# A mixture-of-experts layer takes its tokens by indirect DMA instead of one-hot products

## The chip, the cores and the metric

The kernel runs on one core of one Trainium2 chip. The metric is device time in microseconds (us) of one execution; lower is better. The core has TensorE (PE, with its weight load PEld), VectorE (DVE), ScalarE (ACT), GpSimd (POOL), SyncE (SP) and 16 DMA engines. Each engine works through its own queue in order.

## The reference, cut to what matters

Two transformer blocks with 512 tokens of width 1024 end in a mixture of experts: 32 experts of hidden width 256, and each token goes to two of them. The part that the change touches is this:

```python
g_sel = top_k(g_logits, 1)                       # one of 4 groups
top_val, top_idx = top_k(e_logits_sel, 2)        # two of its 8 experts
gates = sum(one_hot(e_idx, 32) * e_weight)       # 512 x 32
...
a = einsum('nd,edf->nef', hf, w_g); u = einsum('nd,edf->nef', hf, w_u)
hid = silu(a) * u * gates
out = out + einsum('nef,efd->nd', hid, w_d)
```

All inputs are float32. Experts read 100 MB of weights, so each weight passes through the core once.

## The kernel before, in words

The kernel works in float32 accuracy with faster products: each operand is split into a high part (rounded on ACT, line 259, tiles `whi`) and a low part (the rest, on DVE, line 260, tiles `wlo`), three buffers each. Weights come as a stream of 512 KB pieces, called half units here (128 x 1024 floats), issued by SP (lines 234, 241 and 253). An expert has six of them: four for up and gate (`expert_up`, products at line 1589, 128x512) and two for down (`expert_down`, lines 266 to 268).

An expert handles up to `CAP` = 64 tokens. Experts go in groups of `EB` = 4, and in a group in two pairs; a pair fills 128 rows. Eight groups follow one another. For each group, `take(e)` prepares the tokens one group ahead. `gather` compares a table of ranks with a ramp and so writes a one-hot matrix `oh` (DVE, line 1557). It then multiplies the 512 normalised tokens, high and low part, by `oh` on PE: 64 products of 256 columns at line 1569. ACT copies each result from PSUM into `xg`, where the high and the low half of an expert's tokens lie side by side (line 1571, eight copies a group). `slots` multiplies `oh` by a small table `gcol` to learn the token number and the gate of each slot (PE line 1369, then five small DVE steps; the last, line 1382, writes the row numbers `sr` as integers). Those row numbers serve the output: `add_rows` scales the result by the gate and POOL adds it to rows of `out` in DRAM by an indirect DMA (line 1494), two a group.

Between these, `expert_hidden` folds the high and low products (line 1597), applies silu (ACT line 1599) and the product with `u` (DVE line 1600, `hid`); `expert_turn` transposes `hid` on PE (line 1609).

The order within each engine is fixed when the kernel is built, by a scheduler that interleaves the steps which Python yields. A weight tile is loaded as soon as its buffer is free, in the order of the SP queue. `fetch` sets how many half units may be in memory: `RING` = 11 buffers of their own, four in tiles of the residual, and five in pairs of half-size temporaries (line 241), 20 in all. A half unit in two half-size tiles is split by two ops of 512 columns on ACT and two on DVE.

Of the kernel before, what the change touches and what calls it, by code (L numbers as in the profile page):

```python
# [19 lines left out]
D = 1024  # L20
# [33 lines left out]
RING = 11  # L54
# [146 lines left out]
class Ker:  # L201
# [1039 lines left out]
    def route_begin(self):  # L1241
# [3 lines left out]
        for t, name in zip(self.rc, ("w_r", "tri", "b_r", "rdesc")):  # L1245
# [6 lines left out]
                   for n, j in enumerate(XORDER)}  # L1252
        self.ss, self.nr = None, 0

    def route_part(self, k, h):
# [12 lines left out]
        for i in range(NT):  # L1268
            nc.scalar.copy(self.xt[2 * i + k // 4][:, k % 4 * 128:(k % 4 + 1) * 128], pt[:, i * 128:(i + 1) * 128])

    def route(self, p, keep, mid):
# [38 lines left out]
        xt = [{}, {}]  # L1310
        for n, j in enumerate(XORDER):
            xt[0][j] = self.p_x.tile([128, T], F32R, name=("xh", "xl")[n // 4])[:, :512]
            nc.scalar.activation(xt[0][j], self.xt[j], AF.Copy, scale=y[:, 1 + j // 2:2 + j // 2])

        def lows():
            for n, j in enumerate(XORDER):
                xt[1][j] = self.p_x.tile([128, T], F32R, name=("xl", "xh")[n % 2])[:, :512]
                i = V.scalar_tensor_tensor(xt[1][j], self.xt[j], y[:, 1 + j // 2:2 + j // 2], xt[0][j].bitcast(F32), op0=OP.mult,
                                           op1=OP.subtract)
                if n == 0:  # L1320
                    self.tc.keep_in_program_order(i)

        return xt, lows, (lg, gm, og, m1, o1, m2, o2)

    def gating(self, p, found, gall, gcol):
# [29 lines left out]
        V.memset(gcol.bitcast(F32), 0.0)  # L1355
        V.tensor_copy(gcol[:, :, :, 0], self.slot[:, 0:4, None].to_broadcast([128, 4, NEXP // 2]))
        V.tensor_copy(gcol[:, :, :, 1:3], g2)
        V.tensor_sub(gcol[:, :, :, 3:5], g2, gcol[:, :, :, 1:3].bitcast(F32))

    def slots(self, pe, oh, gcol, e):  # L1360


        nc = self.nc
        V = nc.vector
        n = EB // 2
        ps = self.psb()
        for b in range(n):
            for i in range(NT):
                nc.tensor.matmul(ps[:, b * 8:b * 8 + 6], oh[:, i, b * 128:(b + 1) * 128], gcol[:, i, e // 2 + b, :], start=i == 0,
                                 stop=i == NT - 1, skip_group_check=True)  # L1370
        p3 = ps[:, :n * 8].rearrange("p (a b) -> p a b", a=n)
        g = pe.tile([128, n], F32, name="sg")
        t = pe.tile([128, n], F32, name="st")
        r = pe.tile([128, n], I32, name="sr")
        s = pe.tile([128, n, 8], F32, name="sp")
        V.tensor_copy(s[:, :, :5], p3[:, :, :5])
        for j in range(2):
            rows = slice(j * CAP, (j + 1) * CAP)
            V.tensor_add(g[rows], s[rows, :, 1 + j], s[rows, :, 3 + j])
        V.tensor_scalar(t, s[:, :, 0], 0.0, self.slot[:, 4:5], op0=OP.is_equal, op1=OP.mult)  # L1380
        V.scalar_tensor_tensor(t, s[:, :, 0], -1.0, t, op0=OP.add, op1=OP.add)
        V.tensor_copy(r, t)
        return r, g

    def moe(self):
# [3 lines left out]
        with ExitStack() as es:  # L1389
# [5 lines left out]
            gcol = pk.tile([128, 4, NEXP // 2, 6], F32R, name="gcol")  # L1395
# [3 lines left out]
            for n in range(4):  # L1399
# [3 lines left out]
                if n < 2:  # L1403
                    xs.append(pk.tile([128, 8, EB, 2, CAP], F32R, name=f"xg{n}"))
# [24 lines left out]
            xt, lows, found = self.route(pr, (rank, cmax), to_rows)  # L1429
# [20 lines left out]
            for j in range(RING + 4):  # L1450
                fetch(j)
            list(take(0))
            for j in range(RING + 4, RING + 9):
                fetch(j)
# [29 lines left out]
            self.overflow(pe, cmax, rank, gall, xt, xs, hh, out)  # L1484
# [12 lines left out]
    def overflow(self, pe, cmax, rank, gall, xt, xs, hh, out):  # L1497
# [3 lines left out]
        with tc.If(cnt > CAP):  # L1501
# [5 lines left out]
            with tc.For_i(0, NEXP, 1) as e:  # L1507
                with tc.For_i(CAP, S, CAP) as b:
                    oh, steps = self.gather(pe, rank[:, :, bass.ds(e, 1)], iota[:, bass.ds(b, CAP)], xt, xs[0])
                    list(steps)  # L1510
# [39 lines left out]
    def gather(self, pe, rank, iota, xt, x, lows=None):  # L1550

# [7 lines left out]
        if lows:  # L1559
            lows()  # L1560

        def steps():
            for part, src in enumerate(xt):
                for k in range(0, 8, 2):
                    pg = self.psb()
                    for j in range(2):
                        sl = slice((k + j) % 4 * 128, (k + j) % 4 * 128 + 128)
                        for i in range(NT):
                            nc.tensor.matmul(pg[:, j * m:(j + 1) * m], src[2 * i + k // 4][:, sl], oh[:, i, :m], start=i == 0,  # L1569
                                             stop=i == NT - 1, skip_group_check=True)  # L1570
# [549 lines left out]
```

## Time and profile before

| | us |
|---|---|
| median of three runs | 1752.95 (1751.96 to 1754.55) |
| the profiled execution | 1755.02 |
| its span, first to last instruction | 1753.1 |
| PE busy in the span | 1705.3 (97%) |
| DVE busy | 1090.5 (62%) |
| ACT busy | 861.0 (49%) |
| POOL busy | 59.1 (3%) |

Busy shares are means over stages that differ. The expert layer fills the last 310 us of the span, from about 1435 us on; its own shares have to be read from that stretch alone.

### The profile page before, as it was taken

The page shows a single profiled execution, that of the slowest core. Times are in us where ns is not written, and L with a number is a line of the kernel's source. Part 1 is how long each engine was busy: PE and PEld are TensorE (multiplying, and loading weights), DVE is VectorE, ACT ScalarE, POOL GpSimd, SP SyncE. Part 2 cuts the span into 40 slices and gives each one's busy share as a digit, 9 for nine tenths or more (in the row PEclk, how much of TensorE's full clock was granted, in tenths as well). Part 3 has the DMA queues.
Part 4 walks back from the last instruction along what each step waited for, and adds up shares of the span by engine and source line. Part 5 has one row for each costly group of instructions (what it writes and reads, how often), then busy time and mean ns, then how long its engine had stood idle before and what let it go on. Part 6 is the DMA issues. An engine that isn't in the chain of part 4 may idle for free.

```text
span 1753.1 us, 26914 instructions
## 1 busy us (share of the span) xinstructions
PE 1705.3 (97%) x10674; PEld 1497.2 (85%) x10674; DVE 1090.5 (62%) x1885; ACT 861.0 (49%) x1419; POOL 59.1 (3%) x65
## 2 busy tenths in 40 slices
PE   8999999999999999999999999999999999999996
PEld 8999999999999999878888888767767788888884
DVE  7678675633434344553434345589857768999995
ACT  6455654432323134441314144454346359999995
POOL 0000000000000000000000000100000000101102
PEclk9999999999999999999999999999969999999998
DMA  5211113232323222133333234322201458999993
GB/s 189 72 49 49 37 37 105 86 96 85 96 86 96 86 96 74 59 96 97 96 95 92 90 96 143 114 61 72 73 13 55 172 213 299 323 341 358 354 363 89
DMA packets 72339, 223.72 MB, mean 128 GB/s; under 512 B 9464, under 2 KB 9520, under 8 KB 72208
## 3 DMA queue, kind: packets, MB, share of 16 engines
q1 hardware_dynamic: 68976, 215.70, 36.7%
q0 software_dynamic: 3232, 6.25, 1.9%
q8 instruction: 85, 1.39, 0.3%
q14 instruction: 46, 0.38, 0.1%
HBM read 213.50 MB, written 12.60 MB: 129 GB/s over the span
## 4 chain that ended last, share of the span: by engine, by line
PE 91%; DVE 5%; ACT 2%; DMA 1%; issue 1%; SPq 0%; POOL 0%; POOLq 0%; DVEq 0%
PE pm L289 32%; PE ps L289 29%; PE ps L1589 6%; PE ps L1569 3%; PE ps L266 3%; PE ps L267 2%; PE ps L268 2%; PE ps L557 2%; DVE wlo L260 1%; PE ps L2060 1%; PE ps L2035 1%; PE ps L2053 1%; PE pm L485 1%; PE ps L1192 1%; DVE acc L1835 1%
## 5 line engine op out<-in xcount | busy, mean ns | idle before, releaser
L259 ACT CAST whi<-wraw 128x1024 fp32r<-128x1024 f32 (+1 forms) x309 | 321.3, 1045 | 606.1 <-PE pm L289 293.0
L260 DVE TENSOR_TENSOR wlo<-wraw,whi 128x1024 fp32r<-128x1024 f32 (+1 forms) x309 | 373.1, 1216 | 40.9 <-ACT whi L259 30.6
L289 PE MATMUL pm<-xh,whi 128*128 128x264 f32 x976 | 202.1, 288 | 8.4 <-ACT whi L259 6.0
L289 PE MATMUL pm<-xh,wlo 128*128 128x264 f32 x976 | 200.7, 286 | 0.5 <-DVE wlo L260 0.5
L289 PE MATMUL pm<-xl,whi 128*128 128x264 f32 x976 | 200.4, 287 | 0.1
L289 PE MATMUL ps<-xh,whi 128*128 128x512 f32 x472 | 191.8, 407 | 0.0
L289 PE MATMUL ps<-xh,wlo 128*128 128x512 f32 x472 | 186.1, 395 | 0.0
L289 PE MATMUL ps<-xl,whi 128*128 128x512 f32 x472 | 185.3, 393 | 0.0
L289 PEld LDWEIGHTS pm<-xh,whi 128*128 128x128 f32 x976 | 152.7, 190 | 9.4 <-ACT whi L259 6.0
L289 PEld LDWEIGHTS pm<-xh,wlo 128*128 128x128 f32 x976 | 152.4, 189 | 0.8 <-DVE wlo L260 0.7
L289 PEld LDWEIGHTS pm<-xl,whi 128*128 128x128 f32 x976 | 152.0, 189 | 0.7 <-DVE xl L467 0.6
L289 PEld LDWEIGHTS ps<-xh,whi 128*128 128x128 f32 x472 | 89.1, 189 | 23.5 <-issue 1.8
L289 PEld LDWEIGHTS ps<-xh,wlo 128*128 128x128 f32 x472 | 89.0, 189 | 21.0
L289 PEld LDWEIGHTS ps<-xl,whi 128*128 128x128 f32 x472 | 89.2, 189 | 19.5 <-issue 0.5
L1589 PE MATMUL ps<-wlo,xg 128*128 128x512 f32 x256 | 103.8, 405 | 1.3 <-DVE wlo L260 1.2
L289 PE MATMUL pm<-ah,whi 128*128 128x264 f32 x512 | 104.1, 284 | 0.0
L289 PE MATMUL pm<-ah,wlo 128*128 128x264 f32 x512 | 104.0, 285 | 0.0
L289 PE MATMUL pm<-al,whi 128*128 128x264 f32 x512 | 103.7, 284 | 0.0
L1589 PE MATMUL ps<-whi,xg 128*128 128x512 f32 x256 | 103.6, 405 | 0.0
L289 PE MATMUL ps<-ah,whi 128*128 128x512 f32 x256 | 101.1, 395 | 0.0
L289 PE MATMUL ps<-ah,wlo 128*128 128x512 f32 x256 | 101.0, 394 | 0.0
L289 PE MATMUL ps<-al,whi 128*128 128x512 f32 x256 | 100.5, 392 | 0.0
(500 smaller groups left out, 3216.1 us busy)
## 6 DMA issues: line engine op xcount, KB each, us to landing
wraw<-in_stream_dram SPq DMA_DIRECT2D x306, 512.0 KB, 3.7
t<-in_stream_dram SPq DMA_DIRECT2D x90, 256.0 KB, 6.9
h<-in_stream_dram SPq DMA_DIRECT2D x37, 512.0 KB, 5.9
h<-in_xT_dram SPq DMA_DIRECT2D x16, 264.0 KB, 3.3
hd<-h SPq DMA_DIRECT2D x8, 256.0 KB, 2.0
h<-hd SPq DMA_DIRECT2D x8, 256.0 KB, 3.3
out_dram<-t SPq DMA_DIRECT2D x8, 256.0 KB, 2.1
gt<-rbd POOLq DMA_DIRECT2D x4, 256.0 KB, 5.7
```

Source lines behind the costliest of these rows:

```text
L259: self.nc.scalar.copy(hi, src)
L260: i = self.nc.vector.tensor_sub(lo, src, hi.bitcast(F32))
L266: nc.tensor.matmul(ps, wh, xh, start=start, stop=False)
L267: nc.tensor.matmul(ps, wh, xl, start=False, stop=False)
L268: nc.tensor.matmul(ps, wl, xh, start=False, stop=stop)
L289: nc.tensor.matmul(ps, w[:, b, :], x[:, sl], start=(first and f and i == 0), stop=(last and l and i == nb - 1))
L485: nc.tensor.matmul(pm[:, s, :H2], l, r[:, s * H2:(s + 1) * H2], start=i == 0, stop=i == len(pairs) - 1)
L557: nc.tensor.matmul(pa[:, j * 64:(j + 1) * 64], xs, self.second(xs, i), start=True, stop=True)
L1192: nc.tensor.matmul(ps[:, i * 128:i * 128 + n], self.z[:, i, cols], self.bands[i][:, g, :n], start=False, stop=i == NT - 1, skip_group_chec ...
L1569: nc.tensor.matmul(pg[:, j * m:(j + 1) * m], src[2 * i + k // 4][:, sl], oh[:, i, :m], start=i == 0, stop=i == NT - 1, skip_group_check=True)
L1589: nc.tensor.matmul(pa, xk, v[:, k], start=kk == 0 and n == 0, stop=kk == 7 and n == 1, skip_group_check=True)
L1835: nc.vector.match_replace(out=acc, in_to_replace=m8, in_values=acc, imm_value=sel)
```

## The change

The normalised-to-be tokens (before the division by their root mean square) are written once to a DRAM buffer `xr`, 512 rows of 1024 floats, from the tiles into which the router transposes them: four DMAs after the fourth and four after the eighth block. `gather` and its products are gone. In their place `take` does the following for each group: `onehot` writes `oh`; `slot_cols` multiplies it by `gcol`, which has now eight columns and also holds each token's scale in two parts; `slot_rows` makes the row numbers `sr` and the scales `sy`; POOL fetches the two pairs' rows from `xr` by two indirect DMAs (`rows_in`) and multiplies each by its scale (`tensor_scalar`, 128x1024); PE transposes each in eight 128x128 pieces, ACT copies the rounded high part and DVE subtracts it to get the low part (`rows_turn`, two of each per pair). The up-front scaling and splitting of all tokens (16 ops of 128x512) is gone.

`RING` goes from 11 to 9, which makes room for the two row tiles. Eight half units more are held in the buffers of the former token tiles `xh` and `xl`, in halves; so 26 in all.

```diff
-RING = 11
+RING = 9
+AHEAD = RING + 17
...
+        if self.nr % 4 == 0:
+            for i in range(NT):
+                nc.sync.dma_start(self.xr[i * 128:(i + 1) * 128, k // 4 * 512:(k // 4 + 1) * 512], self.xt[2 * i + k // 4])
...
+    def slot_rows(self, pe, s, n):
+
+        V = self.nc.vector
+        t = pe.tile([128, EB // 2], F32, name="st")[:, :n]
+        r = pe.tile([128, EB // 2], I32, name="sr")[:, :n]
+        y = pe.tile([128, EB // 2], F32, name="sy")[:, :n]
+        V.tensor_scalar(t, s[:, :n, 0], 0.0, self.slot[:, 4:5], op0=OP.is_equal, op1=OP.mult)
+        V.scalar_tensor_tensor(t, s[:, :n, 0], -1.0, t, op0=OP.add, op1=OP.add)
+        V.tensor_copy(r, t)
+        V.tensor_add(y, s[:, :n, 1], s[:, :n, 2])
+        return r, y
...
+    def rows_in(self, b, r):
+
+        t = self.xg[b]
+        self.nc.gpsimd.indirect_dma_start(out=t, out_offset=None, in_=self.xr, in_offset=bass.IndirectOffsetOnAxis(ap=r, axis=0),
+                                          bounds_check=S - 1, oob_is_err=False)
+
+    def rows_turn(self, b, x):
+
+        nc = self.nc
+        for k in range(0, 8, 4):
+            pt = self.psb()
+            for j in range(4):
+                nc.tensor.transpose(pt[:, j * 128:(j + 1) * 128], self.xg[b][:, (k + j) * 128:(k + j + 1) * 128], self.ident)
+            p4 = pt.rearrange("p (a e c) -> p a e c", a=4, e=2)
+            hi, lo = (x[:, k:k + 4, :, part, :] for part in range(2))
+            nc.scalar.copy(hi, p4)
+            nc.vector.tensor_sub(lo, p4, hi.bitcast(F32))
+            yield
...
             def take(e):
-                oh, steps = self.gather(pe, rank[:, :, e:e + EB], iota, xt, bufs(e)[0], None if e else lows)
-                yield from steps
+                n = EB // 2
+                oh = self.onehot(pe, rank[:, :, e:e + EB], iota)
+                s = self.slot_cols(pe, oh, gcol, e, n, 0, 8 if e else 4)
+                r, y = self.slot_rows(pe, s, n)
+                for b in range(n):
+                    self.rows_in(b, r[:, b:b + 1])
                 if e == 0:
                     self.gating(pr, found, gall, gcol)
-                places[e] = self.slots(pe, oh, gcol, e)
+                    s = self.slot_cols(pe, oh, gcol, e, n, 4, 8)
+                places[e] = r, self.slot_gates(pe, s)
+                yield
+                for b in range(n):
+                    nc.gpsimd.tensor_scalar(self.xg[b], self.xg[b], y[:, b:b + 1], None, op0=OP.mult)
+                    yield
+                for b in range(n):
+                    yield from self.rows_turn(b, bufs(e)[0][:, :, 2 * b:2 * b + 2])
...
-                n = j % (RING + 9) - RING
+                n = j % AHEAD - RING
...
+                elif n < 12:
+                    self.ahead[j] = self.load_halves(j, [self.p_x.tile([128, T], F32, name=t) for t in ("xh", "xl")])
```

The scheduler places the new steps. Three places matter below. The first is DVE at the start of the second group: `sr` is the row number that the gathers wait for, `hid_13315` and `hid_13319` are the hidden values of that group's first and second expert, and `xs_13303` takes the low part of the next group's tokens. Before, the chain that makes `sr` stood at the group's start and only the output waited for it:

```order
L1376 COPY sp<-ps 128x2x5
L1557 TENSOR_TENSOR oh<-iota,rank 128x1024
L1600 TENSOR_TENSOR hid_13305<-hid_13305,ps 64x256
L1379 TENSOR_TENSOR sg<-sp 64x2 x2
L1380 TENSOR_SCALAR st<-sp,slot 128x2
L260 TENSOR_TENSOR wlo<-wraw,whi 128x1024
L1381 SCALAR_TENSOR_TENSOR st<-sp,st 128x2
```

Now it reads:

```order
L1629 TENSOR_TENSOR hid_13315<-hid_13315,ps 64x256
L1386 TENSOR_TENSOR sg<-sp 64x2 x2
L261 TENSOR_TENSOR wlo<-wraw,whi 128x1024
L261 TENSOR_TENSOR hh_13304<-ps,hh_13301 128x2x64
L261 TENSOR_TENSOR wlo<-wraw,whi 128x1024 x2
L1378 CAST sr<-st 128x2
L261 TENSOR_TENSOR wlo<-wraw,whi 128x1024 x2
L261 TENSOR_TENSOR wlo<-h_92,whi 128x1024
L1629 TENSOR_TENSOR hid_13319<-hid_13319,ps 64x256
L1601 TENSOR_TENSOR oh<-iota,rank 128x1024
L1405 TENSOR_TENSOR xs_13303<-ps,xs_13303 128x4x2x64
```

Between the row numbers and the first subtraction that needs the gathered rows, DVE has three splits, `hid` and `oh`. The second place is POOL over one group: `rows_13295` and `rows_13296` are the row tiles of the two pairs.

```order
L1535 DMA out_dram<-y,sr 512x1024 x2
L1392 DMA rows_13295<-xr,sr 128x1024
L1392 DMA rows_13296<-xr,sr 128x1024
L1474 TENSOR_SCALAR rows_13295<-rows_13295,sy 128x1024
L1474 TENSOR_SCALAR rows_13296<-rows_13296,sy 128x1024
```

The queue held nothing but the additions to `out` before; a group's two gathers now stand behind two of those. The third place is PE in the same group: line 1618 is the up product, 1626 the fold, 1401 the transpose of gathered rows, and 267 to 269 the down products of the group's first expert.

```order
L1618 MATMUL ps<-wlo,xs_13306 128x512
L1626 MATMUL ps<-low_13318,fold 128x512
L1401 MATMUL ps<-c_97,rows_13295 128x128 x4
L267 MATMUL ps<-whi,hh_13301 128x512
L268 MATMUL ps<-wlo,hh_13301 128x512
L269 MATMUL ps<-whi,hh_13304 128x512
```

The transposes stand behind the second expert's fold and ahead of the first expert's down products, so those wait when the rows are late. At the same kind of place before, one-hot products stood, whose operands lay in memory:

```order
L1597 MATMUL ps<-low_13300,fold 128x512
L1569 MATMUL ps<-oh,xh 128x256
L1569 MATMUL ps<-oh,xl 128x256 x8
L1589 MATMUL ps<-whi,xg_13292 128x512
L1589 MATMUL ps<-wlo,xg_13292 128x512
```

Sixty-four of these went per group; now 16 transposes do.

## Rows read from the trace of the kernel before

**Rows 1.** The page: busy time by engine; the chain that ended last, by engine.

```profile
PE 1705.3 (97%) x10674; PEld 1497.2 (85%) x10674; DVE 1090.5 (62%) x1885; ACT 861.0 (49%) x1419; POOL 59.1 (3%) x65
...
PE 91%; DVE 5%; ACT 2%; DMA 1%; issue 1%; SPq 0%; POOL 0%; POOLq 0%; DVEq 0%
```

**Rows 2.** Second to seventh group: us, PE, PEld, DVE, ACT, POOL busy; PEclk, DMA, GB/s.

```profile
1479.80:1516.50 36.70, 36.69 (x197) 31.05 (x198) 33.80 (x46) 34.11 (x53) 4.37 (x2) 1.00 0.98 339
...
1664.06:1700.70 36.64, 36.64 (x197) 30.99 (x198) 33.78 (x46) 34.08 (x53) 4.37 (x2) 1.00 0.97 354
sum 220.90, PE 220.81 PEld 185.61 DVE 202.91 ACT 204.87 POOL 27.02; mean PE 36.80 PEld 30.94 DVE 33.82 ACT 34.14 POOL 4.50
```

**Rows 3.** Groups of instructions in those six groups: count, busy us, mean ns.

```profile
L260 DVE TENSOR_TENSOR wlo<-wraw,whi 128x1024 fp32r<-128x1024 f32 x81 | 96.6, 1219 | 9.0 <-ACT whi L259 8.5
L260 DVE TENSOR_TENSOR wlo<-t,whi 128x512 fp32r<-128x512 f32 x70 | 45.1, 684 | 2.5 <-ACT whi L259 2.1
L260 DVE TENSOR_TENSOR wlo<-h,whi 128x1024 fp32r<-128x1024 f32 x28 | 34.0, 1220 | 4.8 <-ACT whi L259 4.6
...
L1571 ACT CAST xg<-ps 128x512 fp32r<-128x512 f32 x48 | 27.5, 581 | 2.3 <-PE ps L1569 1.9
```

**Rows 4.** DVE in order of time, fifth group: start, us, what.

```profile
1590.34 1.21 DVE L1557 TENSOR_TENSOR oh<-iota,rank 128x1024 fp32r<-128x1024 f32 x1
1591.47 0.41 DVE L1600 TENSOR_TENSOR hid<-hid,ps 64x256 f32<-64x256 f32 x1
1591.81 0.32 DVE L1379 TENSOR_TENSOR sg<-sp 64x2 f32<-64x2 f32 x2
...
1603.91 3.48 DVE L260 TENSOR_TENSOR wlo<-wraw,whi 128x1024 fp32r<-128x1024 f32 x3
...
1618.73 2.50 DVE L260 TENSOR_TENSOR wlo<-t,whi 128x512 fp32r<-128x512 f32 x4
```

**Rows 5.** The chain in order of time, eight gather products.

```profile
1466.00 0.94 PE ps L1569 x8
```

**Rows 6.** DVE subtracting from PSUM, by line, from 1300 us on.

```profile
L1733 DVE TENSOR_TENSOR h<-h,ps 128x512 f32<-128x512 f32 x12 | 8.2, 687 | 8.2 <-PE ps L289 8.1
```

**Rows 7.** DMA issues from 1300 us on (us to landing); then 1740 to 1746.

```profile
h<-hd SPq DMA_DIRECT2D x8, 256.0 KB, 3.3
...
out_dram<-y,sr POOLq DMA_INDIRECT x16, 8.9
...
out_dram<-y,sr POOLq DMA_INDIRECT x1, 5.9
```

**Rows 8.** POOL's indirect DMA: ns min/median/max of the issuing instruction; a POOL fill.

```profile
L1494 POOL DMA_INDIRECT out_dram<-y,sr x16: 1541/2158/7369, 1471.9 to 1742.0; - x16
...
L1413 POOL MEMSET low<- 64x512 f32 x2 | 1.1, 534 | 0.1
```

**Rows 9.** The first group's start, DVE and then PE, in order of time.

```profile
1434.41 1.22 DVE L1557 TENSOR_TENSOR oh<-iota,rank 128x1024 fp32r<-128x1024 f32 x1
...
1442.97 0.34 DVE L1358 TENSOR_TENSOR gcol<-gall,gcol 128x128 fp32r<-128x128 f32 x1
1445.72 0.17 DVE L1376 COPY sp<-ps 128x10 f32<-128x10 f32 x1 [2.41 <-PE ps L1369]
...
1444.73 0.95 PE L1369 MATMUL ps<-gcol,oh 128*128 128x6 f32 x8
1445.54 0.48 PE L1589 MATMUL ps<-whi,xg 128*128 128x512 f32 x1
```

**Rows 10.** The last group: a wait in the chain; DVE's last split and last output.

```profile
1704.03 6.54 DMA wraw<-in_stream_dram
...
1733.50 1.22 DVE L260 TENSOR_TENSOR wlo<-h,whi 128x1024 fp32r<-128x1024 f32 x1
...
1740.46 0.75 DVE L1492 TENSOR_SCALAR y<-ps,sg 128x512 f32<-128x512 f32 x1 [4.30 <-PE ps L268]
```

**Rows 11.** Four us with the stream at its fastest: columns as in rows 2.

```profile
1672.00:1676.00 4.00, 4.00 (x24) 3.40 (x23) 3.64 (x5) 3.98 (x7) 0.86 (x1) 1.00 1.04 410
```

More of the change, by code (lines that the diff above doesn't have):

```diff
@@ L1252, in route_begin @@
                    for n, j in enumerate(XORDER)}
+        self.xr = self.p_d.tile([S, D], F32, name="xr")
         self.ss, self.nr = None, 0
@@ L1309, in route, with token_cols @@
         V.tensor_copy(cmax, cm)
[L1310 to L1323, printed above, removed]
+        return y, (lg, gm, og, m1, o1, m2, o2)
+    def token_cols(self, gcol, y):
+        V = self.nc.vector
+        wide = lambda ap: ap[:, :, None].to_broadcast([128, 4, NEXP // 2])
+        V.tensor_copy(gcol[:, :, :, 0], wide(self.slot[:, 0:4]))
+        V.tensor_copy(gcol[:, :, :, 1], wide(y[:, 1:5]))
+        V.tensor_sub(gcol[:, :, :, 2], wide(y[:, 1:5]), gcol[:, :, :, 1].bitcast(F32))
     def gating(self, p, found, gall, gcol):
@@ L1368, in slots @@
             for i in range(NT):
[L1369 to L1376, printed above, removed]
+                nc.tensor.matmul(ps[:, b * 8 + c0:b * 8 + c1], oh[:, i, b * 128:(b + 1) * 128], gcol[:, i, e // 2 + b, c0:c1],
+                                 start=i == 0, stop=i == NT - 1, skip_group_check=True)
@@ L1377, in slots, with slot_gates @@
+    def slot_gates(self, pe, s):
+        g = pe.tile([128, EB // 2], F32, name="sg")
         for j in range(2):
             rows = slice(j * CAP, (j + 1) * CAP)
[L1379 to L1383, printed above, removed]
+            self.nc.vector.tensor_add(g[rows], s[rows, :, 4 + j], s[rows, :, 6 + j])
+        return g
@@ L1394, in moe @@
             nc.gpsimd.dma_start(iota, self.a["iota"][:, :CAP])
-            gcol = pk.tile([128, 4, NEXP // 2, 6], F32R, name="gcol")
+            gcol = pk.tile([128, 4, NEXP // 2, 8], F32R, name="gcol")
+            nc.vector.memset(gcol.bitcast(F32), 0.0)
+            self.xg = [pk.tile([128, D], F32, name=f"rows{n}") for n in range(EB // 2)]
+            for t in self.xg:
+                nc.gpsimd.memset(t, 0.0)
             gall = pk.tile([128, 4, NEXP], F32, name="gall")
@@ L1483, in moe @@
             self.more_raw = None
-            self.overflow(pe, cmax, rank, gall, xt, xs, hh, out)
+            self.overflow(pe, cmax, rank, gall, gcol, xs, hh, out)
     def add_rows(self, pe, py, place, b, out):
@@ L1508, in overflow @@
                 with tc.For_i(CAP, S, CAP) as b:
-                    oh, steps = self.gather(pe, rank[:, :, bass.ds(e, 1)], iota[:, bass.ds(b, CAP)], xt, xs[0])
-                    list(steps)
+                    oh = self.onehot(pe, rank[:, :, bass.ds(e, 1)], iota[:, bass.ds(b, CAP)])
+                    nc.vector.memset(oh[:, :, CAP:2 * CAP].bitcast(F32), 0.0)
+                    r, y = self.slot_rows(pe, self.slot_cols(pe, oh, gcol, 0, 1, 0, 4), 1)
+                    self.rows_in(0, r)
+                    nc.gpsimd.tensor_scalar(self.xg[0], self.xg[0], y, None, op0=OP.mult)
+                    list(self.rows_turn(0, xs[0][:, :, 0:2]))
                     hu = lambda j: self.hu(idx=e * 6 + j)
@@ L1548, in add_back, with onehot @@
                 nc.vector.tensor_add(d, d, ps)
-    def gather(self, pe, rank, iota, xt, x, lows=None):
+    def onehot(self, pe, rank, iota):
         nc = self.nc
@@ L1558, in gather @@
                                 rank[:, :, :, None].to_broadcast([128, NT, n, CAP]), op=OP.is_equal)
[L1559 to L1570, printed above, removed]
-                    nc.scalar.copy(x[:, k:k + 2, :n, part, :], pg[:, :2 * m].rearrange("p (a e c) -> p a e c", a=2, e=n))
-                    yield
-        return oh, steps()
+        return oh
     def expert_up(self, par, x, c, hu, mid=lambda: None):
```

25 lines of the change are left out of this document (13 added, 12 removed).

## The prediction

> **What bounds the kernel now.** I read the page first. PE is busy 97% of the span, and 91% of the chain that ended last lies on it [rows 1]. On that reading, work taken off PE is time gained. But that is a mean over stages, so I read the expert layer's own stretch, by groups of four experts. From the second to the seventh group PE is busy without a gap, 220.81 us of 220.90, one group every 36.8 us [rows 2]. The reader should see the columns beside it: in the same 36.8 us DVE is busy 33.8 us and ACT 34.1 us, and the DMA engines show 0.97 to 0.98, where 1.04 is what they show at their fastest [rows 2, 11]. So four resources stand within 10% of one another. Relieving one gives no more than the distance to the next.
>
> The next question is what DVE needs if it never waits. Busy time counts 1.22 us for a full split of 1024 columns standing alone [rows 3]. In a run without gaps three take 3.48 us, so the pitch is (3.48 - 1.22) / 2 = 1.13 us; four halves take 2.50 us, so theirs is (2.50 - 0.68) / 3 = 0.60 us [rows 3, 4]. Over the six groups a full split cost 96.6 / 81 = 1.19 us on average [rows 3]. With 18 of them a group, closing the gaps would save 18 x 0.06 = 1.1 us: DVE's floor now is about 32.8 us a group.
>
> **The change part by part.**
>
> *PE.* Eight gather products take 0.94 us [rows 5], so 64 take 7.5 us a group. Sixteen transposes take their place; at the 0.12 us of a gather product they would cost 1.9 us, and I take that. PE then needs 36.8 - 7.5 + 1.9 = 31.2 us and no longer sets the pace.
>
> *ACT.* Eight copies a group go (27.5 / 48 = 0.57 us each [rows 3]), four come, and twelve half casts more replace six full ones, about 1 us. That is a relief of a good 1 us: not the bound either.
>
> *DVE.* It gains four subtractions from PSUM of 512 columns. The nearest row shows 0.69 us alone [rows 6]; in a run I take the halves' pitch, 0.60, so 2.4 us. Half units in half-size tiles were 5 of 20 and are 13 of 26, so of 24 a group 12 come in halves instead of 6: 12 x 0.60 - 6 x 1.13 = 0.4 us. The new scale `sy` is one more small step, 0.2 us. DVE's floor becomes 32.8 + 2.4 + 0.4 + 0.2 = 35.8 us. So of PE's 5.6 us, 1.0 us a group can arrive at most. Seven groups took 1700.7 - 1445.5 = 255.2 us [rows 2, 9], the first 2.5 us less than the others, since three units had been split ahead. After: 7 x 35.8 - 2.5 = 248.1, a gain of 7.1 us.
>
> *The rows' way.* This is the new chain: `sr` on DVE, gather, scale on POOL, transpose, copy, subtraction. The order gives it little cover. From `sr` to the first subtraction DVE has three splits, `hid` and `oh`: 3 x 1.13 + 0.34 + 1.13 = 4.9 us [rows 4]. The chain is longer. No gather stands in the trace. Bounds from issue to landing: 3.3 us for 256 KB from DRAM through SP, 8.9 us for the indirect additions [rows 7]. I take 6.0, near the one addition that met no stream, 5.9 us [rows 7]; its issuing instruction (2.2 us in the median [rows 8]) is work that a gather shares. A scale has no row either; a POOL fill of 512 columns takes 0.53 us [rows 8], so 1.1 us for 1024. Then four transposes 0.5, the copy 0.6, and some 0.1 us for the hand-over between engines: 8.3 us. DVE waits 8.3 - 4.9 = 3.4 us. Ahead of it on PE stand the transposes, and behind them the down products; ACT's copy holds its later casts too. So the wait is nobody's cover. The first group's order puts 6.5 us between (the same pitches) and waits 1.8. Six others and that one: 6 x 3.4 + 1.8 = 22.2 us. The second pair's rows land 2.2 us later, behind 6.6 us more of DVE work, and cost nothing.
>
> *The scales beside DVE.* No row shows POOL computing while DVE works. DVE may lose nothing, or as much as both scales last, 2.1 us a group. Neither end has a nearer row; I take the middle, 1.05 us, 7.4 us over seven groups. Here a rule of the Trainium skill speaks against the change. By the page "SBUF — State Buffer", section "Who interferes with whom", a DVE instruction with two inputs in SBUF, which every weight split is, and a GpSimd instruction that reads SBUF shut each other out for their whole length. By that rule the term would be 14.7 us instead of 7.4; no row here can show it.
>
> *The start.* Before, `oh` ended at 1435.6 and the first up product began at 1445.5, behind 64 gather products and eight slot products of 0.95 us [rows 9]. Now two sets of slot products run, the second behind the gate table (0.34 us), since `sr` stands behind both copies: I get `sr` at 1438.7. Landing at 1444.7, the second pair 2.2 us later, scale 1.1, eight transposes 0.9: the up products begin at about 1449, 3.5 us later. The weights are then all in memory, so this is not given back by DMA.
>
> *The eighth group.* It has no next group to fetch for. It ran from 1700.7 to 1740.5, 39.8 us, with 6.5 us of waiting for weights [rows 2, 10]. With six more units ahead that wait goes. DVE then needs 35.8 less `oh`, the subtractions and small steps (1.1 + 2.4 + 1.2), 31.1, and the end behind its last split is serial, 1733.5 to 1740.5, 7.0 [rows 10]: 38.1, a gain of 1.7 us.
>
> *Costed at nothing:* the 2 MB for `xr` go out while PE still works on the layer before; the last four are issued 10 us ahead of the gathers. If they were late, each us would come onto the start once.
>
> **Sum:** +3.5 - 7.1 + 22.2 + 7.4 - 1.7 = +24.3 us. The profiled execution took 1755.0, 2 us above the median; on the median of 1752.95 this gives **1777 us**. With landing at 8.9 the stall and the start grow by 7 x 2.9 + 2.9 = 23, to 1800; with 3.3 they shrink by 2.7 at eight places, to 1756.
>
> **The rivals.**
>
> *A, gather late,* the forecast: 1765 to 1800. For it: the fixed order and 4.9 us of cover. Against it: landing is bounded, not seen.
>
> *B, the gather hides and DVE is the bound.* It needs the row chain under 4.9 us, or PE and ACT so far behind DVE that the subtraction comes later. Sum without the 22.2: +2, 1755.
>
> *C, B with the scales in full:* POOL's 2.1 us a group all on DVE, whatever the mechanism, 1755 + 7 = 1762. The rule of the page named above is the case for it.
>
> *D, faster.* One mechanism: DVE holds its pitch of 35.8 us because the rows always arrive within its cover and POOL takes nothing from it: 3.5 - 7.1 - 1.7 = -5.3, 1748. It decides where the row chain falls from 8.3 below 4.9 us. The full 5.6 us a group that PE frees (1718) is excluded by DVE's floor, unless its pitches are wrong.
>
> *E, DMA becomes the bound.* 24 units at 410 GB/s take 30.7 us [rows 11]; a group's share of 0.97 at 36.8 us is 34.3 us of full flow [rows 2], so the two additions cost 1.8 us each. Two gathers at that price make 37.9 us a group, 1.0 above B's 36.9: 1762.
>
> **How the numbers follow.** A 0.50, B 0.13, C 0.10, E 0.09, D 0.18. The prediction is A's time. About 0.2%, 3.5 us, is what a measurement of this kernel can tell from no change. D and a little of B are faster: 0.20. Most of B is within: 0.08. The rest, 0.72, is slower. The range runs from within D, 1747, past A's upper bound, 1805; alone, A has 1765 to 1800.
>
> **What the changed profile would show.** A: PE's busy share in the groups falls well below 36 of 37 us, and the largest single idle of DVE, ACT and PE is in the stretch from `sr` to the first subtraction, ended by POOL's scale, with a group period of about 40 us. B: DVE above 97% busy, period near 37. C: splits of far more than 1.22 us, or gaps before them, while POOL scales. E: SP's queue never waits for a buffer. Wrong would be the forecast if gathers land in under 3 us, or if DVE's subtraction costs other than 0.6 to 0.7 us. Right or wrong, line 1569's 7.5 us a group must be gone from PE.

## The result: 111 us slower, and the profile after

The changed kernel takes 1863.85 us (median of four, 1857.01 to 1865.29) against 1752.47 us before (four runs): a ratio of 1.0625, 95% interval 1.0598 to 1.0653. The direction was forecast, the size was not: +111 us in place of +24, outside the range. The profiled execution took 1857.01 us.

The page after, busy time by engine; it answers to [rows 1].

```profile
PE 1694.2 (91%) x10298; PEld 1459.3 (79%) x10298; DVE 1108.9 (60%) x1966; ACT 844.4 (46%) x1425; POOL 138.9 (7%) x99
```

Every engine but DVE and POOL has less to do, and even DVE gained only 18 us. So the time went into waiting. Five groups of the expert layer, from one `sp` copy to the next, in windows whose columns are those of [rows 2]:

```profile
1499.10:1550.45 51.35, 36.55 (x151) 25.86 (x150) 36.76 (x60) 33.45 (x57) 20.39 (x6) 0.87 0.78 273
...
1705.02:1756.16 51.14, 38.15 (x149) 27.34 (x149) 36.89 (x59) 32.73 (x55) 12.55 (x6) 0.83 0.82 267
sum 257.06, PE 182.30 PEld 131.89 DVE 183.64 ACT 164.08 POOL 73.14; mean PE 36.46 PEld 26.38 DVE 36.73 ACT 32.82 POOL 14.63
```

A group takes 257.06 / 5 = 51.4 us, where it took 36.8; DVE is busy 36.7 us of it. Nothing is full any more: PE, DVE, ACT and DMA all have gaps. In DVE's groups of instructions from 1440 us on, two lines hold most of the idle time:

```profile
L1405 DVE TENSOR_TENSOR xs<-ps,xs 128x512 fp32r<-128x512 f32 x32 | 21.9, 686 | 52.9 <-ACT xs L1404 52.9
...
L1378 DVE CAST sr<-st 128x2 int32<-128x2 f32 x7 | 1.2, 167 | 27.3 <-issue 27.3
```

The first is the stall the prediction spoke of: the subtraction waits for rows that come late (11.4 us of the 52.9 stand ahead of the first group, at the start). The second was not in it at all. `sr`, the row numbers, is written by DVE, and DVE stands still 27.3 us before it, in six groups, "issue" being the profile's word for a wait that it cannot name. Before, none of the eight writes of `sr` waited:

```profile
L1382 DVE CAST sr<-st 128x2 int32<-128x2 f32 x8 | 1.3, 159 | 0.0
```

One group of the changed kernel in order of time shows both waits behind each other:

```profile
1607.44 2.45 POOL L1535 DMA_INDIRECT out_dram<-y,sr  x1 [15.87 <-ACT whi L260]
...
1616.13 0.17 DVE L1378 CAST sr<-st 128x2 int32<-128x2 f32 x1 [4.98 <-issue]
...
1617.13 1.38 POOL L1392 DMA_INDIRECT rows<-xr,sr  x1 [7.23 <-DVE wlo L261]
...
1623.22 2.85 POOL L1474 TENSOR_SCALAR rows<-rows,sy 128x1024 f32<-128x1024 f32 x1 [2.42 <-DMA rows<-xr,sr]
...
1626.12 1.11 PE L1401 MATMUL ps<-c,rows 128*128 128x128 f32 x4 [11.90 <-POOL rows L1474]
...
1627.27 0.58 ACT L1404 CAST xs<-ps 128x512 fp32r<-128x512 f32 x1 [12.64 <-PE ps L1401]
...
1627.89 0.69 DVE L1405 TENSOR_TENSOR xs<-ps,xs 128x512 fp32r<-128x512 f32 x1 [6.53 <-ACT xs L1404]
...
1629.83 1.05 ACT L260 CAST whi<-wraw 128x1024 fp32r<-128x1024 f32 x1 [1.98 <-PE ps L269]
...
1630.91 1.23 DVE L261 TENSOR_TENSOR wlo<-wraw,whi 128x1024 fp32r<-128x1024 f32 x1 [2.33 <-ACT whi L260]
```

Read the brackets on DVE: 4.98 + 6.53 + 2.33 = 13.8 us idle, nearly all that this group of 51.9 us has beyond its 36.6 us of DVE work. PE waits 11.9 us in one piece. The third wait is a consequence of the second: DVE waits for ACT's cast, and that cast waited 1.98 us for PE's down products (line 269). After PE's pause of 11.9 us its granted clock is 0.51, the 1.2 GHz level, and only then 1.00, the 2.4 GHz level (windows over the same place, PEclk the third column from the end):

```profile
1626.10:1630.10 4.00, 3.98 (x12) 3.31 (x13) 0.69 (x1) 0.85 (x2) 2.17 (x1) 0.51 0.32 128
1630.10:1634.00 3.90, 3.90 (x22) 3.21 (x21) 2.77 (x3) 3.41 (x5) 0.67 (x1) 1.00 0.17 34
```

Why does `sr` wait? Its tile has two buffers (its pool has `bufs=2`). Before, the row numbers of a group were written as that group began, so two sets were alive at most. Now `take` runs a whole group ahead and writes `sr` early in the group before. The previous group's last addition (`add_rows` runs one expert behind) is then still reading its set. Three sets are alive. The addition above was issued at 1607.44, additions land 8.6 us after their issue in the median, and `sr` was written at 1616.13, which fits. The DMA issues of the changed kernel (count, median us to landing):

```profile
rows<-xr,sr POOLq DMA_INDIRECT x16, 6.2
out_dram<-y,sr POOLq DMA_INDIRECT x16, 8.6
```

### The profile page after: what moved, and what is told of

It reads as the page before. It is cut to its first block, busy times and chain, and to the rows that moved or that the text cites. A ratio compares the mean times of both kernels' runs of the same rounds, so it can differ in the third digit from the quotient of the medians.

```text
span 1855.2 us, 26474 instructions
## 1 busy us (share of the span) xinstructions
PE 1694.2 (91%) x10298; PEld 1459.3 (79%) x10298; DVE 1108.9 (60%) x1966; ACT 844.4 (46%) x1425; POOL 138.9 (7%) x99
## 5 line engine op out<-in xcount | busy, mean ns | idle before, releaser
L260 ACT CAST whi<-wraw 128x1024 fp32r<-128x1024 f32 (+1 forms) x271 | 281.9, 1044 | 626.3 <-PE pm L290 293.3
L261 DVE TENSOR_TENSOR wlo<-wraw,whi 128x1024 fp32r<-128x1024 f32 (+1 forms) x271 | 328.3, 1216 | 41.6 <-ACT whi L260 32.1
L1618 PE MATMUL ps<-wlo,xs 128*128 128x512 f32 x256 | 110.7, 432 | 25.1 <-DVE wlo L261 24.5
L1618 PE MATMUL ps<-whi,xs 128*128 128x512 f32 x256 | 106.0, 414 | 1.9 <-ACT whi L260 1.9
```

Source lines behind the costliest of these rows:

```text
L260: self.nc.scalar.copy(hi, src)
L261: i = self.nc.vector.tensor_sub(lo, src, hi.bitcast(F32))
L1618: nc.tensor.matmul(pa, xk, v[:, k], start=kk == 0 and n == 0, stop=kk == 7 and n == 1, skip_group_check=True)
```

## The experiments

Theory 1 was formed from this trace: two waits in series, each group, the row-number buffer and the late rows with their scale. Its rivals: one of them hides the other, so that removing either alone gives nothing; or the excess is VectorE held up by the scales. All ratios are against the kernel before on the same chip.

| run | what | us | ratio, 95% interval |
|---|---|---|---|
| changed | | 1863.85 | 1.0625 [1.0598, 1.0653] |
| 1 | three `sr` buffers | 1818.77 | 1.0374 [1.0323, 1.0425] |
| 2 | no scales | 1839.99 | 1.0495 [1.0462, 1.0528] |
| 3 | transposes two steps later | 1833.98 | 1.0461 [1.0430, 1.0491] |
| 4 | 1 and 3 | 1783.63 | 1.0174 [1.0118, 1.0229] |
| 5 | 4, no scales | 1767.06 | 1.0090 [1.0073, 1.0107] |
| 6 | 4, scales on ACT | 1804.09 | 1.0294 [1.0277, 1.0312] |
| 7 | 4, scaled once up front | 1766.02 | 1.0085 [1.0068, 1.0102] |
| 8 | 4, 18 ahead | 1776.37 | 1.0149 [1.0131, 1.0168] |
| 9 | 7, 18 ahead | 1763.00 | 1.0063 [1.0046, 1.0080] |
| 10 | 9, outputs scaled on ACT | 1757.52 | 1.0042 [1.0026, 1.0058] |
| 11 | 9, transposes early again | 1796.99 | 1.0254 [1.0234, 1.0273] |
| 12 | 10, 26 ahead once | 1760.66 | 1.0049 [1.0034, 1.0065] |
| 13 | 10, one group gathered | 1756.18 | 1.0017 [1.0003, 1.0030] |
| 14 | 10, two groups' low parts | 1768.75 | 1.0082 [1.0060, 1.0105] |

**1. A third buffer for the row numbers.**

```diff
-        r = pe.tile([128, EB // 2], I32, name="sr")[:, :n]
+        r = pe.tile([128, EB // 2], I32, name="sr", bufs=3)[:, :n]
```

> The row numbers sr get three buffers instead of two; nothing else changes. Theory 1 (each group of the changed kernel loses time at two places one after the other: DVE's write of sr waits for the indirect addition that still reads the old row numbers, 27.3 us in six waits, and PE, ACT and DVE wait for gather plus scale): the 27 us go, 1863.9 becomes about 1837, and the wait before the subtraction stays at about 50 us in all. Rival (the sr wait only shows early what the gather would show later, since POOL and the DMA are what is late): under 8 us change. Rival (the scales on POOL are what costs): no change.

It takes 45 us off, more than the 27.3 us of the wait. Among PE's and DVE's instructions of this run the wait in front of `sr` is gone; the transposes' wait is 47.8 us, where it was 73.7:

```profile
L1401 PE MATMUL ps<-c,rows 128*128 128x128 f32 x128 | 26.2, 327 | 47.8 <-POOL rows L1474 47.8
...
L1378 DVE CAST sr<-st 128x2 int32<-128x2 f32 x8 | 1.3, 161 | 0.0
```

So the other wait did not stay as it was, which the expectation had said. DVE's waits at the subtraction and at the splits, first of the changed kernel, then of this run (us in total, times, longest):

```profile
DVE xs L1405 <- ACT xs L1404: 52.9, 11, 11.4
...
DVE wlo L261 <- ACT whi L260: 23.4, 19, 2.3
```

```profile
DVE wlo L261 <- ACT whi L260: 30.1, 14, 5.5
...
DVE xs L1405 <- ACT xs L1404: 28.2, 7, 11.5
```

Their sum falls from 76.3 to 58.3 us, by 18.0; with the 27.3 that is the 45. The expectation's "nothing else changes" holds for the source and not for the order. With two buffers `sr` could only stand behind the previous group's last output, which still reads the old row numbers; with three the scheduler places `sr` and the gathers ahead of that addition. One group in order of time, to set beside the one at 1607.44 above:

```profile
1593.03 0.16 DVE L1378 CAST sr<-st 128x2 int32<-128x2 f32 x1
...
1594.02 1.57 POOL L1392 DMA_INDIRECT rows<-xr,sr  x1 [7.42 <-PE ps L269]
...
1597.65 1.96 POOL L1535 DMA_INDIRECT out_dram<-y,sr  x1 [0.30 <-issue]
...
1607.11 1.23 DVE L261 TENSOR_TENSOR wlo<-wraw,whi 128x1024 fp32r<-128x1024 f32 x1 [5.43 <-ACT whi L260]
1608.32 0.69 DVE L1405 TENSOR_TENSOR xs<-ps,xs 128x512 fp32r<-128x512 f32 x1
```

Between `sr` and the subtraction DVE now has 8.7 to 10.6 us of work in the six groups, where it had 4.8 to 5.9. So 45 us is the price of the missing buffer as a whole: the wait, and the tight order that it forced. How the 18 us divide between the longer cover and what restarts late behind a wait (PE's clock, ACT's casts) is not separated.

**2. No scales.** The two `tensor_scalar` on POOL are left out.

```diff
-                    nc.gpsimd.tensor_scalar(self.xg[b], self.xg[b], y[:, b:b + 1], None, op0=OP.mult)
```

> The two scales per group on POOL are left out, so the tokens go unscaled into the experts. Theory 1: only the first scale of a group (2.85 us instead of the 1.1 that I had taken) lies in the chain, and both do at the start: 7 x 2.9 + 5.7, about 26 us less, 1838. Rival (POOL's scale shuts DVE's splits out for its whole length, as a term of its own): 2 x 2.85 x 8, 45 us less or more, about 1818, and DVE's splits beside the scales longer than 1.22 us in the changed kernel. Rival (DMA bound): no change.

24 us come off, and both waits remain, the rows now waited for directly at the DMA (waits: us in total, times, longest):

```profile
PE ps L1401 <- DMA rows<-xr,sr: 53.7, 9, 9.6
...
DVE sr L1378 <- issue: 29.1, 6, 6.1
```

So the gather itself, without any scale, comes too late for its place.

**3. Transposes two steps later.** `take` yields twice more between the scales and the transposes.

```diff
                     yield
+                yield
+                yield
                 for b in range(n):
                     yield from self.rows_turn(b, bufs(e)[0][:, :, 2 * b:2 * b + 2])
```

> Two empty steps between scales and transposes: the gathered rows are transposed about half an expert later in PE's order, and everything else is as in the changed kernel. Theory 1: the 41 us that DVE waits for the subtraction outside the first group shrink to under 15, and PE's half clock behind them goes too: 30 to 45 us less, about 1825. The sr wait of 27 us stays. Rival (sr wait and gather wait are one): the sr wait grows by what the other loses, under 10 us change.

30 us come off; the wait for row numbers stays (29.0 us in six), so the rival falls. The waits at the subtraction shrink less than expected: to 30.5 us with the 11.4 at the start, 19.1 without, where under 15 was expected.

**4. Both.**

> Both edits: three buffers for sr and the two empty steps. Theory 1: the two add up, 60 to 75 us less than the changed kernel, about 1795, and what is left against the kernel before is the later start (10 us) and a DVE whose floor is 36 us a group. Rival (DMA is the bound behind the waits): no better than 1815, with the DMA engines above 0.95 in the groups.

80 us come off, against 45 + 30 = 75 apart: the two edits add up, neither wait hides the other, and the rival falls. A group is now 38.9 us, and DVE is busy 37.5 us of it. POOL and DVE now run side by side, and the trace prices what no row before could. POOL's line, then one group in order of time:

```profile
L1474 POOL TENSOR_SCALAR rows<-rows,sy 128x1024 f32<-128x1024 f32 x16 | 65.3, 4087 | 21.7 <-DMA rows<-xr,sr 21.7
```

```profile
1585.42 9.55 POOL L1474 TENSOR_SCALAR rows<-rows,sy 128x1024 f32<-128x1024 f32 x2 [2.40 <-DMA rows<-xr,sr]
1586.55 3.19 DVE L261 TENSOR_TENSOR wlo<-wraw,whi 128x1024 fp32r<-128x1024 f32 x2
...
1593.07 2.39 DVE L261 TENSOR_TENSOR wlo<-wraw,whi 128x1024 fp32r<-128x1024 f32 x2
```

A scale that took 2.85 us alone takes 4.1 us on average and here 4.8. Two splits that begin inside the first take 3.19 us, where two that begin inside the second take 2.39 and two ahead of both 2.35. Both engines lose, POOL more.

**5. The fourth without scales.** The same line is left out as in 2.

> On the fourth experiment, with both waits covered, the two POOL scales are left out, so the experts' inputs are not scaled. Theory 1: with the waits gone VectorE is the bound, and beside a busy VectorE a scale takes 4.1 us on POOL in place of 2.85 and lengthens the VectorE splits that lie beside it (1.26 us mean in place of 1.22). Seven groups of about 38.9 us come down to about 37, and the first take loses its 5.7 us of scales: about 1764 us. Rival: the scales only sit in the cover; the 2 us that VectorE idles in a group come from elsewhere, and only the first take gains: about 1778 us.

16.6 us come off; run 4's two executions lie 7 us apart, so the shares below hold to a few us. First the splits of the fourth run from 1440 us on, then of this one:

```profile
L261 DVE TENSOR_TENSOR wlo<-wraw,whi 128x1024 fp32r<-128x1024 f32 x69 | 85.0, 1261 | 1.5 <-ACT whi L260 1.3
...
L261 DVE TENSOR_TENSOR wlo<-xh,whi 128x512 fp32r<-128x512 f32 x56 | 39.4, 704 | 2.9 <-ACT whi L260 2.9
```

```profile
L261 DVE TENSOR_TENSOR wlo<-wraw,whi 128x1024 fp32r<-128x1024 f32 x69 | 82.0, 1215 | 2.0 <-ACT whi L260 1.6
...
L261 DVE TENSOR_TENSOR wlo<-xh,whi 128x512 fp32r<-128x512 f32 x56 | 38.1, 680 | 0.0
```

Over the five groups of weight splits at line 261, equal in number, the sums are 243.6 and 237.6 us: the scales lengthened DVE by 6.0 us. The first up product comes 3.6 us earlier (1449.75 against 1453.37). Of the 7 us that are left, most seem to be rows that still came late behind slow scales: behind the start, the fourth's PE waited 17.3 - 11.5 = 5.8 us more for them.

**6. Scales on ScalarE.**

```diff
-                    nc.gpsimd.tensor_scalar(self.xg[b], self.xg[b], y[:, b:b + 1], None, op0=OP.mult)
+                    nc.scalar.activation(self.xg[b], self.xg[b], AF.Copy, scale=y[:, b:b + 1])
```

> On the fourth experiment, the two scales go from POOL to ScalarE (as an activation that copies with a scale); the computation is whole. Theory 1: a scale on ScalarE is about 1.05 us, as its copies of 128x1024 are, and holds nobody else; ScalarE is 33 us busy of 39, so it takes the 2.1 us: between the fourth experiment and the one without scales, about 1768 us. Rival: a scale stands in ScalarE's queue and waits there for its gather, the splits behind it are late and VectorE and TensorE with them: 1783 us or more.

The rival holds (1804 us). The scale is 1.15 us there, but it waits for the gather in the queue that all weight splits pass (ACT's waits):

```profile
ACT rows L1474 <- DMA rows<-xr,sr: 42.9, 10, 17.5
```

**7. Scaled once, ahead of the write.**

```diff
-        if self.nr % 4 == 0:
-            for i in range(NT):
-                nc.sync.dma_start(self.xr[i * 128:(i + 1) * 128, k // 4 * 512:(k // 4 + 1) * 512], self.xt[2 * i + k // 4])
...
         _, y = self.rstd(self.ss, S, row=False)
+        for j in XORDER:
+            nc.scalar.activation(self.xt[j], self.xt[j], AF.Copy, scale=y[:, 1 + j // 2:2 + j // 2])
+            nc.sync.dma_start(self.xr[j // 2 * 128:(j // 2 + 1) * 128, j % 2 * 512:(j % 2 + 1) * 512], self.xt[j])
```

> On the fourth experiment, the tokens are scaled once, on ScalarE, as soon as the route knows their scale, and only then written to DRAM; nothing is scaled in a group, and the computation is whole. Theory 1: the groups are those of the experiment without scales; the eight copies (about 5 us on ScalarE) and eight writes lie beside the route's work on VectorE, and the start loses little: about 1766 us. Rival: the writes land late, the first gather waits for them, and the start is 6 us or more later: 1772 us or more. If the groups keep to 36 us, a third possibility is 1752 us, level with the kernel before.

As theory 1 had it, it equals the run without scales, and its first up product comes at 1446.92. Five of its groups:

```profile
sum 192.00, PE 174.81 PEld 123.08 DVE 182.63 ACT 167.11 POOL 32.99; mean PE 34.96 PEld 24.62 DVE 36.53 ACT 33.42 POOL 6.60
```

**8. 18 half units ahead**, without the eight in the former token tiles.

```diff
-AHEAD = RING + 17
+AHEAD = RING + 9
...
-                elif n < 12:
-                    self.ahead[j] = self.load_halves(j, [self.p_x.tile([128, T], F32, name=t) for t in ("xh", "xl")])
```

> On the fourth experiment, the eight half units in the tiles that the route leaves are no longer fetched ahead: 18 in place of 26. Theory 1: VectorE bounds the groups, and DMA, busy 0.95 to 1.0 of a group, only just keeps up; the eight half units (4 MB, 12 us at 345 GB/s) are a store of weights that the groups draw down, so without it DMA becomes the bound late in the run: up to 12 us more, about 1792 us. Rival: they are never drawn on, or the transfers were slower only because there was nothing to fetch: no change, 1784 us.

Theory 1 falls: it is no slower. The median is 7 us less, but the intervals overlap, so the rival's "no change" is not excluded. The eight half units bring nothing here. The splits of 512 columns fall from 182 to 100 and 41 wide ones stand in their place; at the prediction's pitches that is 41 x (1.20 - 1.13) = 2.9 us less for DVE.

**9 to 11.** The ninth joins 7 and 8. The tenth also moves the second half of each output's scaling:

```diff
-        nc.vector.tensor_scalar(y[:, 512:], py[1], g[:, b:b + 1], None, op0=OP.mult)
+        nc.scalar.activation(y[:, 512:], py[1], AF.Copy, scale=g[:, b:b + 1])
```

> The seventh and the eighth experiment together: scaled once before the write, 18 half units ahead, three buffers of row numbers, transposes two steps later; the computation is whole. Theory 1: VectorE bounds a group, and a half unit that comes as two 512 wide pieces costs it more than one 1024 wide piece, whatever the scales do; so the 7 us of the eighth experiment come off again, and the sum is 1766 less 7, 1759 us. Rival: those 7 us came from scales that fell elsewhere; without scales 18 ahead is 1766 us, or more if the store of weights now matters.

> The ninth experiment with the second half of every output pair's scaling on ScalarE too (16 operations of 0.75 us taken from VectorE, which leaves ScalarE with 16 of about 0.69 more). Theory 1: VectorE bounds the groups, so up to 12 us come off the ninth experiment, less what ScalarE, about 35 us busy of 36, makes late: 1752 us, level with the kernel before. Rival: ScalarE and VectorE stand in one chain (copy, then subtraction), and ScalarE is as full: no change or more, 1759 to 1765 us.

The eleventh is the ninth without the two late steps:

```diff
-                yield
-                yield
```

> The ninth experiment with the transposes at the changed kernel's own place again, two steps earlier; only the gather's landing has to be hidden now, no scale. Theory 1: the gather is issued 0.8 us behind the row numbers and lands some 6 us later, against a cover of 5.1 us: with the hand-overs a stall of 2 to 3 us in each of seven groups, 1759 + 17 = about 1776 us. This is the stall the prediction priced, without the scale. Rival: without scales the landing fits into the cover and the time is that of the ninth, 1759 us.

The ninth is 3 us under the seventh (1759 expected, 1763 measured) and the tenth 5.5 us under the ninth (1752 expected, 1757.5 measured); each step's intervals overlap, but seventh and tenth are apart. The eleventh is 34 us over the ninth, twice the 17 us expected, 4.9 us for each of seven groups: that is the price of the gather's latency alone where the transposes come two steps earlier. It is not the changed kernel's place: with three buffers, run 11 has 7.1 to 8.4 us of DVE work between `sr` and the subtraction in six of the groups. In the group shown here the rows arrive 6.5 us after the gather's issue at 1540.60, itself 0.9 us behind `sr` (PE, in order of time):

```profile
1547.14 0.41 PE L1401 MATMUL ps<-c,rows 128*128 128x128 f32 x2 [2.60 <-DMA rows<-xr,sr]
```

**12. The store of 26 once.** The tenth, with the eight half units fetched only at the start.

```diff
+STORE = AHEAD + 8
...
-                n = j % AHEAD - RING
+                n = (j if j < STORE else (j - STORE) % AHEAD) - RING
```

> The tenth experiment with the eight half units in the tiles that the route leaves fetched ahead once (26 at the start), after which those tiles are used no more and the rotation is the tenth's of 18; the computation is whole. Theory 1: with the waits gone DMA is the bound beside VectorE (its share is 1.00 to 1.03 in every 40 us of the tenth experiment from 1500 on, and VectorE's busy time falls from 38.6 to 35.6 of 40 as the store is drawn down), and a store of 4 MB more is 11 us of its time at 370 GB/s, while only eight half units cost VectorE two 512 wide splits in place of one wide one (1 to 2 us): the span falls by up to 9 us, to about 1749 us, just under the kernel before. Rival: VectorE with ScalarE alone is the bound, DMA is busy only because it has room: 1757 to 1760 us.

No gain, as the rival said: 1.0049 against 1.0042. A larger store is not what is missing.

**13 and 14. DMA or VectorE?** In 13 only the first group's rows are gathered, in 14 only the first two groups' low parts are subtracted.

```diff
-                for b in range(n):
+                for b in range(n if e == 0 else 0):
                     self.rows_in(b, r[:, b:b + 1])
```

> The tenth experiment, but only the first group's rows are gathered; the later groups work on those same rows, so 14 gathers of 512 KB (7.3 MB, 20 us of DMA at 370 GB/s) are left out. If DMA limits the groups once the waits are gone, the time falls by 10 to 20 us, to about 1742 us. If VectorE with ScalarE limits them, it stays at 1755 to 1758 us.

```diff
-            nc.vector.tensor_sub(lo, p4, hi.bitcast(F32))
+            if low:
+                nc.vector.tensor_sub(lo, p4, hi.bitcast(F32))
...
+                    yield from self.rows_turn(b, bufs(e)[0][:, :, 2 * b:2 * b + 2], e < 2 * EB)
```

> The tenth experiment, but the low part of the tokens is subtracted only in the first two groups; the later ones use an old low part, so 24 VectorE operations at a pitch of 0.60 us (14 us) are left out. If VectorE limits the groups, the time falls by 8 to 14 us, to about 1747 us. If DMA limits them, it stays at 1755 to 1758 us.

One group of the tenth and the same group of 13:

```profile
1521.99:1557.84 35.85, 33.41 (x148) 23.76 (x147) 34.64 (x50) 32.24 (x50) 13.03 (x4) 1.00 1.02 372
```

```profile
1521.34:1557.21 35.87, 33.45 (x148) 23.78 (x147) 34.66 (x51) 32.27 (x50) 3.08 (x2) 1.00 1.01 359
```

Without gathers the group is as long, the time (1756.18 us) is the one expected if DMA is not the limit, and the DMA share is still 1.01 while fewer bytes move. So in run 10 DMA is not the limit, and its share near 1 is no sign of one. Run 14 went against both its expectations. The groups in which DVE lost work alternate:

```profile
1521.08:1560.91 39.83, 33.61 (x145) 25.29 (x145) 31.36 (x46) 31.42 (x49) 11.04 (x4) 0.91 0.98 346
1560.91:1596.07 35.16, 32.60 (x143) 22.88 (x142) 30.37 (x46) 31.16 (x50) 6.05 (x4) 1.00 1.00 368
1596.07:1637.92 41.85, 38.16 (x157) 26.38 (x157) 35.39 (x51) 34.89 (x54) 6.12 (x4) 0.96 0.97 344
```

DVE's busy time fell (from 34.3 to 32.0 us in the mean of five groups), and the time rose. DVE's splits waited 34.0 us for ACT's casts, where they waited 13.1 us in the tenth. Without the subtraction the scheduler placed other instructions differently: in the group that starts near 1560 us, ACT casts two full `h` pieces ahead of the first copy of rows in the tenth, and in run 14 half a piece `t`. What that costs is not separated; so this run does not name the limit. It shows only that DVE work can go without time going.

## Why the prediction was wrong, point by point

- **PE's work** left as forecast: line 1569 is gone, and PE no longer sets the pace. The 128 transposes were busy 22.0 us in run 5, 0.17 us each where 0.12 was taken. PE's busy time did not fall to 31.2 us a group, though: it is 35.0 in run 7 and 33.5 in run 10, in part because a product that stands behind a gap is counted longer (the up products of the low part take 430 ns in the mean of run 7's groups, 403 before).
- **The rows' way, the step that failed.** It says: "This is the new chain: `sr` on DVE, gather, scale on POOL, transpose, copy, subtraction." It began at `sr` and took the writing of `sr` itself as free. It asked what waits for the new transfer, not what the moved write has to wait for. That term was missing whole: DVE stood still 27.3 us for it, and run 1, which gives the tile a third buffer, takes 45 us off. The 4.9 us of cover were read rightly, but from an order in which the two buffers were already built in; with three, run 1 has 8.7 to 10.6. The additions' 8.9 us [rows 7] and the order that put `sr` a group earlier were both in view; what was not counted were the live sets of a tile with two buffers. Neither of the prediction's own signs of being wrong came (gathers landed in 6.2 us, the subtraction took 0.69).
- **The stall's size.** The mechanism was right: in the groups, the longest idle of PE, ACT and DVE stands where the prediction put it, ended by POOL's scale. It was mis-sized. In the group shown, 11.8 us pass from `sr` to the subtraction (1616.13 to 1627.89), not 8.3, and 10.6 to 11.8 in the six groups: landing 6.1 after the issue (6.0 taken), scale 2.85 (1.1 from a POOL fill), 1.0 from `sr` to the gather's issue (0.1 taken), four transposes at half clock 1.15 (0.5). The landing came near only in these groups, whose DMA share is 0.80 in the mean; in run 10, at 1.02, the median is 7.8. The cover was right, 4.8 to 5.9 against 4.9 us. The stall is thus 4.6 to 6.6 us, not 3.4, and it costs more than itself: in run 11, without any scale, the prediction's chain of 8.3 - 1.1 = 7.2 us would have been covered by the 7.1 to 8.4 us of DVE work there, and the place still cost 4.9 us a group. What the prediction left out is that PE resumes at the 1.2 GHz level and ACT's casts start late behind it; both are seen in the trace, their share is not separated.
- **The scales beside DVE** were sized at +7.4, the middle between 0 and 14.7. In the changed kernel itself the term is not there: its splits take 1218 ns as before (1219), because the scales run while DVE waits. Runs 4 and 5, with rows on time, show 6.0 us of longer splits; that this is near the middle of two bounds is luck. The Trainium skill, page "SBUF — State Buffer", section "Who interferes with whom", calls the port pair that DVE and GpSimd share an exclusive lock, for which a DVE instruction with two inputs in SBUF contends with a GpSimd instruction that reads SBUF; the prediction took from it that each shuts the other out while it lasts, 14.7. The trace agrees that they hold each other up, but not for a whole instruction: in the 9.55 us of run 4's two scales DVE is busy throughout and begins six full splits, four of them in the rows shown. The larger part falls on POOL: its scale goes from 2.85 to 4.09 us.
- **The start** was +3.5; the first up product comes 8.1 us later (1453.62 against 1445.54), though `oh` began 2.1 us earlier. In order of time:

```profile
1432.26 1.22 DVE L1601 TENSOR_TENSOR oh<-iota,rank 128x1024 fp32r<-128x1024 f32 x1
...
1437.96 0.16 DVE L1378 CAST sr<-st 128x2 int32<-128x2 f32 x1
...
1439.06 1.17 POOL L1392 DMA_INDIRECT rows<-xr,sr  x1 [50.35 <-DMA xh<-in_stream_dram]
...
1446.25 5.69 POOL L1474 TENSOR_SCALAR rows<-rows,sy 128x1024 f32<-128x1024 f32 x2 [4.70 <-DMA rows<-xr,sr]
1449.16 1.97 PE L1401 MATMUL ps<-c,rows 128*128 128x128 f32 x8 [11.32 <-POOL rows L1474]
```

  `sr` to scale takes 8.3 us (6.0 taken), two scales 5.7, and the transposes run at half clock. Run 7, with nothing to scale, starts at 1446.92.
- **DVE's floor of 35.8 us** gave a gain of 7 us that is not there. The floor itself was near: with both waits and the scales gone (run 7) DVE is busy 36.5 us a group. But it does not run without gaps, and the group takes 38.4. Only with DVE's output work moved too (run 10) does a group come to 36.1 us, and the kernel to 1.0042.
- **The eighth group and what was costed at nothing.** The 1.7 us for a larger store of weights rest on a row that was misread. The 6.54 us at 1704.03 [rows 10] are a piece of the chain that runs through a transfer, not a wait of the engines: in those 6.54 us PE is busy 6.21, DVE 6.18 and ACT 6.31. From the seventh group's last `hid` to ScalarE's last output pass 38.5 us before and 37.4 in the changed kernel, but 38.6 in run 4 with the same store and 37.7 in run 8 without it; so no run shows that the store gives this, and runs 8 and 12 show no gain from it in the time. The writes of `xr` were no cost: the last was issued at 1422.1 us, 17 us ahead of the first gather at 1439.1, and they land in some 3 to 4 us.
- **Rivals.** D (faster) falls: with rows on time and POOL idle the kernel is still 0.85% slower. C's time, 1762, is near runs 5 and 7, which scale nothing in the groups, so not for its reason. E falls for run 10 by run 13; in the changed kernel itself the DMA share is only 0.80. B, with DVE as the bound, describes the rest best, but its sign, DVE above 97% busy, is not met (34.3 of 36.1 us in run 10, 95%), and run 14 speaks against DVE as the only bound, so what holds the last 0.4% stays open.

So the 111 us are, in the order in which the runs took them away (changed, runs 1, 4, 7): 45 the row-number buffer with the order that it forced, 35 the late rows behind it, 18 the scales, and 14 that remain. PE's relief could not pay for them, since DVE and ACT stood only 3 us a group behind it [rows 2]; 8.5 of the 14 went with fewer halves and the output work moved off DVE (runs 9 and 10). No version here beats the kernel before.

## What to carry to other kernels

When a producer is moved a stage earlier, count how many of its results are alive at once, down to the last DMA that reads them, and give its tile that many buffers; a write that waits on a two-buffer tile shows in a profile only as idle "issue" time. After such an edit read the order again before you call the gain the price of the wait: here a third buffer ended 27 us of waiting, moved the write and the gathers up, and took 45 us off. And take the work off the resource that is full only as far as the next one is empty.

## What the runs showed of the hardware that was not expected

- A `tensor_scalar` on GpSimd over 128x1024 floats takes 2.85 us beside an idle VectorE (changed kernel) and 4.1 us in the mean beside a busy one (run 4), while a pair of VectorE splits that begins inside it took 2.39 to 3.19 us, against 2.35 elsewhere. ScalarE does the same work in 1.15 us (run 6).
- An indirect gather of 512 KB landed 6.2 us after its issue in the median of the changed kernel and in 6.7 to 7.8 us in runs 1 to 12; an indirect addition in 7.9 to 9.0 us. In the changed kernel, row numbers that an addition reads were written anew only 7.0 to 8.8 us after the addition's issue.
- The DMA share of a group was 1.02 with the gathers, at 372 GB/s, and 1.01 without them, at 359 GB/s (runs 10 and 13), at the same time.
